# A two-layer trunk on one core: both token halves in one 512-column product, and a rebuilt start

## The chip, the cores and the metric

The kernel runs on one core of a Trainium2 chip. The metric is the device time of one execution in microseconds. Before the change it is 1028.43 us, the median of three runs (1027.76 to 1029.43). The engines are named as in the profile: PE multiplies matrices (PEld is its loading of the stationary operand), DVE and ACT work elementwise, POOL does a few small things, and SP issues most of the transfers.

## The reference, cut to what matters

There are 256 tokens of width 1024 and two layers. Each layer is a feed-forward block, a mixer with two kinds of attention, and a second feed-forward block. All of it is float32.

```
mod = silu(c) @ ada_w[l] + ada_b[l]            # nine rows of 1024 per layer: shift, scale, gate
h = rmsnorm(x, norm_pre[l, 0]) * (1 + sc1) + sh1
y = (silu(h @ w_gate) * (h @ w_up)) @ w_down    # 1024 -> 2816 -> 1024
x = x + 0.5 * g1 * rmsnorm(y, norm_post[l, 0])
# then the mixer with sh2, sc2, g2, then the second feed-forward block with sh3, sc3, g3
```

## The kernel before

**Products.** A float32 value is split into a high part `hi` and a rest `lo`, and a product of two such values is made of three products of the split parts (`mm3`, L476 to L478, and `mm3t`, L484 to L486). In `mm3` 128 tokens are stationary and 512 columns of a weight block move. In `mm3t` 128 columns of a weight block are stationary and the 256 tokens move: weight hi by tokens hi (L484), weight hi by tokens lo (L485), weight lo by tokens hi (L486). The transposed tokens lie in two tiles `hTh` and `hTl`. Every weight block comes by DMA into a `raw` tile and is split in pieces by ACT (`hi`, L437) and DVE (`lo`, L438).

**A feed-forward block** (`ffn`). Its first 512 hidden columns are made with `mm3` from `rows_of`, one token half at a time; in the very first block the loop at the program's start does it. The other 2304 come in nine steps `j` of 256 columns. A step takes a gate block and an up block of 1024 x 256 each, and for both makes 2 x 8 triples of 256-column products into one PSUM tile (`w_a` or `w_b`). Then ACT takes silu of the gate tile (L640), DVE multiplies it by the up tile (L641), and ACT and DVE split the result (L634, L635). The down products (`mm3`, 24 per 256 hidden columns) run between. PSUM has eight tiles: two of each of the tags `w0`, `w1`, `a` and `b`.

**Modulation in the background.** The rows of `ada_w` that are not needed at once are streamed behind the main work. DVE sums them by the values of silu(c) (L501), PE adds over the partitions (L519 and the line before it).

**The start.** Shift and scale of the first block are needed before any real product. They come in four quarters `q` of 256 columns: for each, a shift block and a scale block of 1024 x 256 are loaded (`eraw`). For each, PE makes 16 products that go to 32 partitions each (L959), DVE adds the bias row (L962), one product with `sel` adds up and spreads to all partitions (L963), DVE scales and shifts the tokens (L971, L972), PE transposes them (L591), ACT and DVE write `hTh` (L594) and `hTl` (L595), and 24 products of the first weight blocks follow. Until then PE runs products that nobody uses (`warm`, L937), in numbers given by `WARM`.

**Order.** Nothing of the order is left to the program text. `keep_order` builds the dependences, plays the program forward with a length for every instruction (`cost`), goes backward from the end for due times, repeats this a few times, and fixes the best order found on each engine, SP's queue of transfers included. Numbers in `shift` and `START_ORDER` move whole groups.

Of the kernel before, what the change touches and what calls it, by code (L numbers as in the profile page):

```python
# [11 lines left out]
F32R = mybir.dt.float32r  # L12
# [3 lines left out]
P = 128  # L16
D = 1024
# [13 lines left out]
START_ORDER = ['s0 x0 s1 c0 g0 x1 c1 f0 s2 f1', 'c2 g1 f2 s3 c3 f3', '', '', '']  # L31
WARM = [2, 5, 2]
# [18 lines left out]
def cost(ins, eng, slots):  # L51
# [3 lines left out]
    if kind == "InstDMACopy":  # L55
        return 4 * free * ins.outs[0].ap[0][1] / 360
# [17 lines left out]
    return 264 if kind == "InstTensorScalarPtr" else 464  # L74


def keep_order(tc, nc, slots, shifts):
# [20 lines left out]
    for k, ins in enumerate(L):  # L98
        touch = []
        for w, lst in ((False, ins.ins), (True, ins.outs)):  # L100
            for x in lst:
# [5 lines left out]
                lo = 0 if space == "PSUM" else b.offset if space == "DRAM" else b.offset % row  # L107
                hi = 1 << 30
                if space != "PSUM":
                    hi = lo + 1 + sum(abs(s) * (c - 1) for s, c in (ap if space == "DRAM" else ap[1:]))  # L110
                touch.append((w, name, lo, hi))
# [184 lines left out]
def trunk(ctx, tc, x, c, rel_bias, ada_w, ada_b, norm_pre, norm_post, w_gate, w_up,  # L296
# [125 lines left out]
    def load(shape, srcs):  # L422
        raw = praw.tile([P, 2048], F32, tag="raw", name=nm("raw"))
        rv = raw.rearrange("p (a b) -> p a b", a=shape[0])
# [4 lines left out]
    def unit(key, shape, src, uses=1):  # L429

        if key not in units:
# [3 lines left out]
            for z in range(sec["split"]):  # L435
                sl = slice(z * 2048 // sec["split"], (z + 1) * 2048 // sec["split"])
                nc.scalar.activation(hi[:, sl], raw[:, sl], AF.Copy)  # L437
                nc.vector.tensor_sub(lo[:, sl], raw[:, sl], hi[:, sl].bitcast(F32))  # L438
            units[key] = [uses, hi.rearrange("p (a b) -> p a b", a=shape[0]),
                          lo.rearrange("p (a b) -> p a b", a=shape[0])]  # L440
# [38 lines left out]

    def mm3t(ps_, kt, wt, sl, start, stop):  # L480

        wh, wl = wt[0][:, kt, sl], wt[1][:, kt, sl]
        hh, hl = hT[0][:, :, kt, :], hT[1][:, :, kt, :]
# [93 lines left out]
    hT = [ctile([P, 2, KT, P], f"hT{n}", F32R) for n in "hl"]  # L577
# [8 lines left out]
    def to_T(h, k0, nk, src, turned=False):  # L586
# [5 lines left out]
        hi, lo = (hT[n][:, h, k0:k0 + nk, :] for n in range(2))  # L592
# [51 lines left out]
    def rows_of(h, pair, get):  # L644

        for p_, g in zip(pair, get):
            for q in range(2):
                w = g(q)
                for k in range(4):
                    kt = q * 4 + k  # L650
                    mm3(p_, hT[0][:, h, kt, :], hT[1][:, h, kt, :], w, k, slice(0, 512), kt == 0, kt == 7)
# [8 lines left out]
    def ffn(l, i, first):  # L660
# [21 lines left out]
        for j in range(9):  # L682
# [365 lines left out]
```

## Time and profile before

| | |
|---|---|
| median of three runs | 1028.43 us |
| profiled execution | 1027.23 us |
| its span | 1025.5 us |
| PE, PEld busy | 1005.2, 893.9 us |
| DVE, ACT, POOL busy | 800.5, 553.5, 42.0 us |
| DMA read | 259.76 MB, 254 GB/s over the span |

The span reaches from the first to the last instruction; 1.7 us of the execution lie outside it. Busy times are the union of an engine's instructions; a product of PE is shown longer than its distance to the next, since products are pipelined.

### The profile page before, as it was taken

Reading aid. Unit: us, or ns where it says so; the run is one execution under the profiler, and the core shown is the slowest. Engines: PE = TensorE matmul, PEld = TensorE weight load, DVE = VectorE, ACT = ScalarE, POOL = GpSimd, SP = SyncE. Lnnn points to the kernel's source line nnn. Section 1 sums busy time; section 2 is a strip of 40 time slices with the busy share of each in tenths; the row PEclk is TensorE's granted clock in tenths of the full one; section 3 lists DMA queues with packets and bytes.
Section 4 is the critical chain, followed back from the end, with each engine's and each line's share of the span. In section 5 each row is a group of like instructions: output and inputs, shape, how many; then the busy total and the mean of one; then the engine's idle time right before and its main releaser. Section 6 shows DMA issues by size and latency. Waiting matters only on the chain. (4 is left out here: it accounts for less than half of the span.)

```text
span 1025.5 us, 17316 instructions
## 1 busy us (share of the span) xinstructions
PE 1005.2 (98%) x6514; PEld 893.9 (87%) x6514; DVE 800.5 (78%) x1493; ACT 553.5 (54%) x1250; POOL 42.0 (4%) x80
## 2 busy tenths in 40 slices
PE   7999999999999999999999999999999999999997
PEld 3699998978887899999979999998798779999996
DVE  4799888978887898798889888886879788555542
ACT  2456443665677665555465445444477766544431
POOL 1000000020002000000010000000100110000000
PEclk9999999999999999999999999999999999999999
DMA  9999998958994588898839887886589638555511
GB/s 328 365 361 325 313 284 295 343 175 279 311 306 168 207 291 295 285 316 311 290 122 308 298 290 284 303 288 226 168 301 323 209 127 272 193 181 189 184 64 41
DMA packets 171855, 261.95 MB, mean 255 GB/s; under 512 B 6396, under 2 KB 107484, under 8 KB 171772
## 3 DMA queue, kind: packets, MB, share of 16 engines
q1 hardware_dynamic: 171616, 260.78, 75.3%
q8 instruction: 51, 0.84, 0.3%
q14 instruction: 32, 0.26, 0.1%
q10 hardware_dynamic: 156, 0.07, 0.0%
HBM read 259.76 MB, written 1.07 MB: 254 GB/s over the span
## 5 line engine op out<-in xcount | busy, mean ns | idle before, releaser
L438 DVE TENSOR_TENSOR lo_a<-raw_a,hi_a 128x512 fp32r<-128x512 f32 (+1 forms) x540 | 294.1, 593 | 43.9 <-issue 23.4
L437 ACT ACTIVATE hi_a<-raw_a 128x512 fp32r<-128x512 f32 (+1 forms) x540 | 259.9, 547 | 123.3 <-PE w_a L485 25.7
L484 PE MATMUL w_a<-hTh,hi_a 128*128 128x256 f32 x768 | 218.9, 285 | 0.6 <-ACT kz_a L733 0.6
L485 PE MATMUL w_a<-hTl,hi_a 128*128 128x256 f32 x768 | 217.8, 284 | 0.0
L486 PE MATMUL w_a<-hTh,lo_a 128*128 128x256 f32 x768 | 217.3, 283 | 0.0
L484 PEld LDWEIGHTS w_a<-hTh,hi_a 128*128 128x128 f32 x768 | 147.1, 192 | 2.2 <-ACT kz_a L733 0.8
L485 PEld LDWEIGHTS w_a<-hTl,hi_a 128*128 128x128 f32 x768 | 147.1, 192 | 1.2 <-issue 0.3
L486 PEld LDWEIGHTS w_a<-hTh,lo_a 128*128 128x128 f32 x768 | 147.0, 191 | 0.4
L485 PE MATMUL w_b<-hTl,hi_b 128*128 128x256 f32 x512 | 144.8, 283 | 0.0
L484 PE MATMUL w_b<-hTh,hi_b 128*128 128x256 f32 x512 | 144.8, 283 | 0.0
L486 PE MATMUL w_b<-hTh,lo_b 128*128 128x256 f32 x512 | 144.7, 283 | 0.0
L437 ACT ACTIVATE hi_b<-raw_b 128x512 fp32r<-128x512 f32 (+1 forms) x224 | 105.1, 544 | 71.3 <-DMA raw_b<-in_ffn_w_up_dram 16.5
L438 DVE TENSOR_TENSOR lo_b<-raw_b,hi_b 128x512 fp32r<-128x512 f32 (+1 forms) x224 | 119.9, 588 | 22.9 <-issue 17.1
L484 PEld LDWEIGHTS w_b<-hTh,hi_b 128*128 128x128 f32 x512 | 98.1, 192 | 1.0
L485 PEld LDWEIGHTS w_b<-hTl,hi_b 128*128 128x128 f32 x512 | 98.1, 192 | 0.9
L486 PEld LDWEIGHTS w_b<-hTh,lo_b 128*128 128x128 f32 x512 | 98.1, 192 | 0.2
L501 DVE SCALAR_TENSOR_TENSOR acc_a<-araw_a,ccol,acc_a 128x512 f32<-128x512 f32 x110 | 82.2, 747 | 12.5 <-DMA araw_a<-in_ada_w_dram 11.0
L477 PE MATMUL a_b<-lo_a,str_a 128*128 128x512 f32 x156 | 60.8, 392 | 0.0
L476 PE MATMUL a_b<-hi_a,str_a 128*128 128x512 f32 x156 | 60.3, 392 | 0.0
L478 PE MATMUL a_b<-hi_a,str_a 128*128 128x512 f32 x156 | 60.2, 390 | 0.0
L501 DVE SCALAR_TENSOR_TENSOR acc_b<-araw_b,ccol,acc_b 128x512 f32<-128x512 f32 x46 | 34.5, 749 | 6.4 <-DMA araw_b<-in_ada_w_dram 5.5
L478 PE MATMUL w_b<-hi_a,hTl 128*128 128x512 f32 (+1 forms) x96 | 36.5, 380 | 0.0
(245 smaller groups left out, 1723.8 us busy)
## 6 DMA issues: line engine op xcount, KB each, us to landing
araw_a<-in_ada_w_dram SPq DMA_DIRECT2D x84, 512.0 KB
raw_a<-in_ffn_w_down_dram SPq DMA_DIRECT2D x30, 1024.0 KB
raw_a<-in_ffn_w_gate_dram SPq DMA_DIRECT2D x26, 1024.0 KB
raw_a<-in_ffn_w_up_dram SPq DMA_DIRECT2D x26, 1024.0 KB
araw_b<-in_ada_w_dram SPq DMA_DIRECT2D x44, 512.0 KB
raw_a<-in_mix_w_in_dram SPq DMA_DIRECT2D x18, 1024.0 KB
raw_b<-in_ffn_w_gate_dram SPq DMA_DIRECT2D x16, 1024.0 KB
raw_b<-in_ffn_w_up_dram SPq DMA_DIRECT2D x16, 1024.0 KB
```

Source lines behind the costliest of these rows:

```text
L437: nc.scalar.activation(hi[:, sl], raw[:, sl], AF.Copy)
L438: nc.vector.tensor_sub(lo[:, sl], raw[:, sl], hi[:, sl].bitcast(F32))
L476: nc.tensor.matmul(ps_, hh, wh, start=start, stop=False)
L477: nc.tensor.matmul(ps_, hh, wl, start=False, stop=False)
L478: nc.tensor.matmul(ps_, hl, wh, start=False, stop=stop)
L484: nc.tensor.matmul(ps_, wh, hh, start=start, stop=False)
L485: nc.tensor.matmul(ps_, wh, hl, start=False, stop=False)
L486: nc.tensor.matmul(ps_, wl, hh, start=False, stop=stop)
L501: nc.vector.scalar_tensor_tensor(acc[:, :n], raw[:, t, :], ccol[:, k:k + 1], b if t == 0 else acc[:, :n], op0=ALU.mult, op1=ALU.add)
```

## The change

Four things are edited.

1. `hTh` and `hTl` become one tile `hT`, in which the high and the low part of a 128-row slice lie side by side. The new `mm2t` multiplies weight hi by both at once (512 columns), and weight lo by the high part (256 columns). The two sums lie in two halves of a PSUM tile of their own for each 128 hidden columns; ACT copies the one half out, DVE adds the other. It is used in all steps `j` of the four feed-forward blocks but the very first one.
2. At the start the first quarter of modulation is summed with 16 products that write all 128 partitions, with no `sel` product and no DVE addition; its four half blocks are loaded by themselves.
3. The gate and up block of step `j` = 0 of the first block are loaded in quarters at the start (`b0` to `b3`), and multiplied with each quarter of the tokens as it comes. Their two PSUM tiles (`ahead`) are held from the start on. `WARM` falls from 2, 5, 2 to 2, 3, 0.
4. `cost` gets other lengths for products, transfers and POOL's instructions, and `keep_order` sees strided accesses more finely, so that the order changes everywhere. The memsets of the mixer's key tile are cut in four.

```diff
-START_ORDER = ['s0 x0 s1 c0 g0 x1 c1 f0 s2 f1', 'c2 g1 f2 s3 c3 f3', '', '', '']
-WARM = [2, 5, 2]
+START_ORDER = ['s0 x0 s1 c0 g0 x1 c1 f0 b0 s2 f1', 'b1 c2 g1 f2 s3 c3', 'b2 f3', 'b3', '']
+WARM = [2, 3, 0]
...
-            return max(free, 256) / 2.4 + 2.5
-        whole = max(4 * free / 2.4 + 4, 160)
+            return free / 2.4 + 13.5
+        whole = max(4 * free / 2.4 + 8, 222)
...
+    def mm2t(ps_, k, wt, sl):
+        for kt in range(k):
+            wh, wl = wt[0][:, kt, sl], wt[1][:, kt, sl]
+            both = lambda **f: nc.tensor.matmul(ps_, wh, hTa[:, kt], **f)
+            if kt < k - 1:
+                both(start=kt == 0, stop=False)
+            nc.tensor.matmul(ps_[:, :256], wl, hT[0][:, kt], start=False, stop=False)
+            if kt == k - 1:
+                both(start=kt == 0, stop=True)
...
-            pair = (wps(), wps())
-            for p_, (tag, ws) in zip(pair, (("g", w_gate), ("u", w_up))):
-                w = u_both(l, f, ws, tag, j)
-                for t in range(2):
-                    for k in range(KT):
-                        mm3t(p_[:, t * 256:(t + 1) * 256], k, w, slice(t * P, (t + 1) * P), k == 0, k == KT - 1)
-            act = split(swiglu(*pair), 512)
+            if first and j == 0:
+                hm = swiglu(*ahead)
+            else:
+                gu = []
+                for b, (tag, ws) in enumerate((("g", w_gate), ("u", w_up))):
+                    w = u_both(l, f, ws, tag, j)
+                    gu.append(st())
+                    for t in range(2):
+                        p_ = wps(b)
+                        mm2t(p_, KT, w, slice(t * P, (t + 1) * P))
+                        dst = gu[b][:, t * 256:(t + 1) * 256]
+                        nc.scalar.activation(dst, p_[:, 256:], AF.Copy)
+                        nc.vector.tensor_add(dst, p_[:, :256], dst)
+                nc.scalar.activation(gu[0], gu[0], AF.Silu)
+                nc.vector.tensor_mul(gu[0], gu[0], gu[1])
+                hm = gu[0]
+            act = split(hm, 512)
...
+            if q == 0:
+                nc.tensor.matmul(both, sel[0:1, :], fl(brow0[0:1, 0]), start=True, stop=False)
             for z in range(2):
                 for k in range(KT):
+                    if q == 0:
+                        nc.tensor.matmul(both[:, z * 256:(z + 1) * 256], ccol[:, k:k + 1].to_broadcast([P, P]),
+                                         pre[q][z][:, k, :], start=False, stop=z == 1 and k == KT - 1)
+                        continue
...
+        with shift(START_NEXT):
+            for n in range(2):
+                for t in range(2):
+                    for k in range(2):
+                        kt = q * 2 + k
+                        wh, wl = (w[i][:, n * 2 + k, t * P:(t + 1) * P] for i in range(2))
+                        p_ = ahead[n][:, t * 256:(t + 1) * 256]
+                        nc.tensor.matmul(p_, wh, hT[0][:, kt], start=kt == t == 0, stop=False)
+                        nc.tensor.matmul(p_, wh, hT[1][:, kt], start=False, stop=False)
+                        nc.tensor.matmul(p_, wl, hT[0][:, kt], start=False, stop=kt == 7 and t == 1)
```

The start on PE, before: `a_b` from `gb` and `x` are the unused products, `eraw` are modulation blocks, `hi` and `lo` the first weight block.

```order
L937 MATMUL a_b_138<-gb,ident 128x512 x2
L364 MATMUL w_a_110<-ident,c_105 128x8
L937 MATMUL a_b_138<-x_119,ident 128x512 x5
L959 MATMUL w_a_203<-eraw_a_148,ccol 32x256 x8
L959 MATMUL w_a_203<-eraw_a_153,ccol 32x256 x8
L963 MATMUL w_a_204<-st_a_221,str_a_139 128x512
L937 MATMUL a_b_138<-x_120,ident 128x512
L591 MATMUL w_a_227<-ident,st_a_224 128x128
L959 MATMUL w_a_290<-eraw_a_151,ccol 32x256 x8
L591 MATMUL w_a_227<-ident,st_a_224 128x128
L937 MATMUL a_b_138<-x_120,ident 128x512
L476 MATMUL a_a_135<-hi_a_232,hTh 128x512
```

The same place after the change.

```order
L981 MATMUL a_b_137<-gb,ident 128x512
L376 MATMUL w_a_110<-ident,c_105 128x8
L981 MATMUL a_b_137<-gb,ident 128x512
L981 MATMUL a_b_137<-x_119,ident 128x512 x3
L1005 MATMUL w_a_205<-erow_a_144,str_a_138 128x512
L1009 MATMUL w_a_205<-eraw_a_147,ccol 128x256 x8
L1009 MATMUL w_a_205<-eraw_a_153,ccol 128x256 x8
L618 MATMUL w_a_226<-ident,st_a_223 128x128 x2
L618 MATMUL w_b_258<-ident,st_b_255 128x128 x2
L489 MATMUL a_a_134<-hi_a_231,hT 128x512
L490 MATMUL a_a_134<-lo_a_232,hT 128x512
L491 MATMUL a_a_134<-hi_a_231,hT 128x512
```

The first quarter's products write 128 partitions and are followed by the transposes of both token halves; the second quarter's first block (`eraw_a_151`) no longer stands ahead of the first real product.

ACT at the start after the change: `raw_a_161` is the first weight block, `raw_a_164` the first quarter `b0`, `hT` the transposed tokens.

```order
L627 ACTIVATE junk,ss_a_186<-x_119 128x512 x2
L627 ACTIVATE junk,ss_a_196<-x_120 128x512 x2
L450 ACTIVATE hi_a_231<-raw_a_161 128x512 x4
L450 ACTIVATE hi_a_275<-raw_a_164 128x256 x2
L621 ACTIVATE hT<-w_a_226 128x2x128
L621 ACTIVATE hT<-w_b_258 128x2x128
```

The tokens' `hT` now stands behind all four pieces of the first weight block and the gate half of `b0`; before, two pieces of the first block stood ahead of it.

PE in a step `j` of the first feed-forward block, before: one hidden tile `w_a_902`, three products a slice.

```order
L484 MATMUL w_a_902<-hTh,hi_a_906 128x256
L485 MATMUL w_a_902<-hTl,hi_a_906 128x256
L486 MATMUL w_a_902<-hTh,lo_a_907 128x256
L484 MATMUL w_a_902<-hTh,hi_a_906 128x256
L485 MATMUL w_a_902<-hTl,hi_a_906 128x256
```

PE in such a step after the change.

```order
L498 MATMUL w_b_1140<-hT,hi_b_1111 128x512
L501 MATMUL w_b_1140<-hT,lo_b_1112 128x256
L498 MATMUL w_b_1140<-hT,hi_b_1111 128x512
L501 MATMUL w_b_1140<-hT,lo_b_1112 128x256
L498 MATMUL w_b_1140<-hT,hi_b_1111 128x512
```

Two products a slice take the place of three, with as many columns in all.

DVE beside that, after the change: L726 is the new addition, L451 the splitting of weight blocks, L526 the background sums.

```order
L726 TENSOR_TENSOR st_b_1139<-w_b_1140,st_b_1139 128x256
L451 TENSOR_TENSOR lo_a_1231<-raw_a_1228,hi_a_1230 128x512 x3
L726 TENSOR_TENSOR st_b_1070<-w_b_1090,st_b_1070 128x256
L526 SCALAR_TENSOR_TENSOR acc_a_1387<-araw_b_1437,ccol,acc_a_1387 128x512
L726 TENSOR_TENSOR st_b_1139<-w_b_1159,st_b_1139 128x256
```

The additions are strewn between the splits and the sums; each stands for one PSUM tile.

## Rows read from the trace of the kernel before

**Rows 1.** The page: engine, busy us, share of the span, instructions.

```profile
PE 1005.2 (98%) x6514; PEld 893.9 (87%) x6514; DVE 800.5 (78%) x1493; ACT 553.5 (54%) x1250; POOL 42.0 (4%) x80
```

**Rows 2.** Windows: length, busy us (instructions) by engine, clock, DMA share, GB/s.

```profile
0.00:19.00 19.00, 14.41 (x72) 5.77 (x72) 5.38 (x11) 5.88 (x13) 3.50 (x15) 1.00 0.96 314
19.00:22.00 3.00, 2.25 (x21) 1.08 (x21) 2.92 (x7) 0.67 (x2) 0.00 (x0) 1.00 1.06 379
22.00:64.00 42.00, 42.00 (x271) 32.60 (x271) 34.11 (x62) 21.20 (x41) 0.29 (x1) 1.00 1.06 359
64.00:221.00 157.00, 156.06 (x1055) 144.13 (x1054) 136.16 (x213) 80.21 (x152) 2.01 (x4) 1.00 0.92 314
...
341.00:520.00 179.00, 178.54 (x1202) 165.31 (x1201) 156.53 (x354) 100.30 (x282) 1.77 (x4) 1.00 0.84 285
...
534.00:716.00 182.00, 181.91 (x1216) 168.38 (x1217) 149.09 (x235) 90.03 (x170) 2.19 (x4) 1.00 0.83 287
...
835.00:1004.00 169.00, 168.60 (x1156) 156.79 (x1155) 97.80 (x156) 77.71 (x142) 0.71 (x2) 1.00 0.52 175
```

**Rows 3.** PE's waits in 64:221: who for whom, us, times, longest.

```profile
PE w_a L519 <- DVE ast_a L517: 0.9, 1, 0.9
```

**Rows 4.** The same in 341:520.

```profile
PE w_b L591 <- DVE st_b L613: 0.5, 1, 0.5
```

**Rows 5.** The page's groups: busy us, mean ns.

```profile
L484 PE MATMUL w_a<-hTh,hi_a 128*128 128x256 f32 x768 | 218.9, 285 | 0.6 <-ACT kz_a L733 0.6
...
L484 PE MATMUL w_b<-hTh,hi_b 128*128 128x256 f32 x512 | 144.8, 283 | 0.0
```

**Rows 6.** Timeline of PE in 100:112: start us, us.

```profile
99.70 0.40 PE L476 MATMUL a_b<-hi_a,str_a 128*128 128x512 f32 x1
...
105.15 0.28 PE L484 MATMUL w_b<-hTh,hi_b 128*128 128x256 f32 x1
...
108.98 0.28 PE L486 MATMUL w_b<-hTh,lo_b 128*128 128x256 f32 x1
```

**Rows 7.** Timeline of DVE in 350:372.

```profile
349.64 4.44 DVE L438 TENSOR_TENSOR lo_a<-raw_a,hi_a 128x256 fp32r<-128x256 f32 x13
```

**Rows 8.** Lines of DVE, 256 columns from PSUM: busy us, mean ns, idle before.

```profile
L972 DVE TENSOR_TENSOR st_a<-st_a,w_a 128x256 f32<-128x256 f32 x4 | 1.7, 421 | 0.1
```

**Rows 9.** The same of ACT.

```profile
L817 ACT ACTIVATE st_a<-w_a 128x256 f32<-128x256 f32 x16 | 6.1, 380 | 4.6 <-PE w_a L815 4.6
```

**Rows 10.** DVE's waits in 64:221.

```profile
DVE acc_a L501 <- DMA araw_a<-in_ada_w_dram: 4.9, 4, 3.1
DVE acc_b L501 <- DMA araw_a<-in_ada_w_dram: 3.8, 3, 2.4
DVE lo_a L438 <- ACT hi_a L437: 3.5, 2, 2.0
```

**Rows 11.** DVE's waits in 341:520.

```profile
DVE st_a L641 <- PE w_a L486: 5.3, 4, 3.0
```

**Rows 12.** Timeline of all engines in 0:22.

```profile
6.56 4.56 PE L937 MATMUL a_b<-x,ident 128*128 128x512 f32 x10
...
11.14 1.93 PE L959 MATMUL w_a<-eraw_a,ccol 128*32 128x256 f32 x32
...
13.97 1.10 PE L963 MATMUL w_a<-st_a,str_a 128*128 128x512 f32 x2 [0.90 <-DVE st_a L962]
...
17.18 1.07 PE L959 MATMUL w_a<-eraw_a,ccol 128*32 128x256 f32 x16
...
18.54 0.39 ACT L594 ACTIVATE hTh<-w_a 128x256 fp32r<-128x256 f32 x1
...
18.98 0.61 PE L476 MATMUL a_a<-hi_a,hTh 128*128 128x512 f32 x1
...
20.71 1.07 PE L959 MATMUL w_a<-eraw_a,ccol 128*32 128x256 f32 x16
...
21.71 0.63 ACT L437 ACTIVATE hi_a<-raw_a 128x512 fp32r<-128x512 f32 x1 [0.51 <-DMA raw_a<-in_ffn_w_up_dram]
...
21.71 0.50 PE L476 MATMUL a_b<-hi_a,hTh 128*128 128x512 f32 x1
```

More of the change, by code (lines that the diff above doesn't have):

```diff
@@ L55, in cost @@
     if kind == "InstDMACopy":
-        return 4 * free * ins.outs[0].ap[0][1] / 360
+        run = 1
+        for step, n in reversed(list(ins.ins[0].ap)):
+            if step != run and n > 1:
+                break
+            run *= n
+        return 4 * free * ins.outs[0].ap[0][1] / (348 if run <= 256 else 388 if run <= 512 else 415)
     if kind == "InstMatmult":
@@ L106, in keep_order @@
                 ap, space = list(x.ap), slots[name][2]
[L107 to L111, printed above, removed]
+                if space == "PSUM":
+                    touch.append((w, name, 0, 1 << 30))
+                    continue
+                lo = b.offset if space == "DRAM" else b.offset % row
+                dims = [(s, c) for s, c in (ap if space == "DRAM" else ap[1:]) if c > 1]
+                starts = [lo]
+                while len(dims) > 1 and dims[0][0] > 0 and len(starts) * dims[0][1] <= 16:
+                    s, c = dims.pop(0)
+                    starts = [v + s * n for v in starts for n in range(c)]
+                low, size = sum(min(0, s * (c - 1)) for s, c in dims), sum(abs(s) * (c - 1) for s, c in dims)
+                touch += [(w, name, v + low, v + low + size + 1) for v in starts]
         for w, name, lo, hi in touch:
@@ L429, in unit @@
     def unit(key, shape, src, uses=1):
+        size = shape[0] * shape[1]
         if key not in units:
@@ L575, in rstd_of @@
         return r2
-    hT = [ctile([P, 2, KT, P], f"hT{n}", F32R) for n in "hl"]
+    hTa = ctile([P, KT, 2, 2, P], "hT", F32R)
+    hT = [hTa[:, :, n] for n in range(2)]
     def back(t):
@@ L896, in ada_load @@
         raw = (plo if m else phi).tile([P, KT, 256], F32, tag="lo" if m else "hi", name=nm("eraw"))
-        nc.sync.dma_start(raw, rows(ada_w[0], 0, KT)[:, :, m * D + q * 256:m * D + (q + 1) * 256])
+        n = KT // 2 if q == 0 else KT
+        for k in range(0, KT, n):
+            nc.sync.dma_start(raw[:, k:k + n], rows(ada_w[0], k * P, n)[:, :, m * D + q * 256:m * D + (q + 1) * 256])
         return raw
@@ L908, in load_first, with load_next @@
         loaded["first", q] = load((4, 512), first_srcs(q))
+    def load_next(q):
+        loaded["next", q] = load((4, 256), [(slice(n * 2, n * 2 + 2), rows(w[0, 0], q * 256, 2)[:, :, 512:768])
+                                            for n, w in ((0, w_gate), (1, w_up))])
     def load_mod(q, m):
@@ L939, in trunk @@
     warm(WARM[0], gb)
+    ahead = (wps(0), wps(1))
     rx, xg = [None, None], [[None, None], [None, None]]
@@ L960, in trunk @@
                                      pre[q][z][:, k, :], start=k < 4, stop=k >= 4)
-            t = st()
-            nc.vector.tensor_add(t, parts, fl(brow0[:, q]))
-            nc.tensor.matmul(both, sel, t, start=True, stop=True)
+            if q:
+                t = st()
+                nc.vector.tensor_add(t, parts, fl(brow0[:, q]))
+                nc.tensor.matmul(both, sel, t, start=True, stop=True)
         cq = slice(q % 2 * 256, q % 2 * 256 + 256)
```

37 lines of the change are left out of this document (22 added, 15 removed).

## The prediction

> **What bounds the kernel now.** I read the page's busy times first, then windows by stage, then PE's waits, then timelines. PE is busy 98% of the span and DVE 78% [rows 1]. The windows show what the share hides: in the four feed-forward stages (64 to 221, 341 to 520, 534 to 716, 835 to 1004) PE is busy for all but 0.1 to 0.9 us, while DVE is busy 136.16 of 157, 156.53 of 179, 149.09 of 182 and 97.80 of 169 us [rows 2]. PE's waits there are one of 0.9 us in the first stage and one of 0.5 in the second [rows 3, 4]. So in these stages time is what PE's products take, one after another; DVE is next, with 21, 22, 33 and 71 us of room. From 22 to 64 PE is busy too, 42.00 of 42 us, with DMA at a share of 1.06; only before 22 does PE wait for data [rows 2].
>
> **The new product.** A product's cost is its distance to the next, not its shown duration. From 99.70 to 105.15 there are 24 products of 512 columns, 227.1 ns each; from 105.15 to 108.98 32 distances of 256-column products, 119.7 ns each [rows 6]. A line through the two gives 0.4195 ns a column and 12.3 ns that every product pays. A triple of three products costs 359.1 ns now and 227.1 + 119.7 = 346.8 after: 12.3 ns less. There are 768 + 512 = 1280 triples [rows 5]; 128 of the mixers and the 32 of the first step `j` = 0 keep the old form, which leaves 1120. 1120 x 12.3 ns = 13.8 us off PE (3.1 in the first stage, 3.5 in each of the other three). Since PE has no other time to lose there, this is also on the path. The columns stay the same; that a 512-column product takes 227 ns with the tokens moving and the weights stationary no row shows. Bounds: if it costs as much as 512 columns do in two pieces, 239.4 ns, nothing is gained; if it costs what the line gives without the fixed part, 214.8 ns, 27.6 us are. I take 227.1, a row of the same engine, type and size.
>
> The row puts the fixed part of a product at 12.3 ns. The Trainium skill, page "TensorE: Matmul & The Clock Gate", section "Back-to-back issue gap", gives columns divided by 2.4 plus about 2.5 ns for a product at full clock. This trace does not agree: it would be 109 ns where the rows have 119.7. By the page the term would be 1120 x 2.5 ns = 2.8 us.
>
> **What the new form adds.** For each of the 2 x 2 tiles of a step ACT copies 256 columns out of PSUM and DVE adds 256: 32 tiles in the first stage, 36 in each of the others, 140 in all. DVE's 13 pieces of 256 columns took 4.44 us, 0.335 apart and 0.42 the last [rows 7]; from PSUM the duration is the same, 0.421 [rows 8]. So 10.7 us more on DVE in the first stage and 12.1 in the others, 47 in all. ACT's copy of this size takes 0.380 [rows 9], 12 to 14 us a stage; ACT is busy about half of every stage [rows 2], so it costs nothing by occupancy. The silu and the multiplication stay one each.
>
> Does DVE hold it? Room after the addition and PE's shorter stage: 20.8 - 10.7 - 3.1 = 7.0 us, 22.5 - 12.1 - 3.5 = 6.9, 32.9 - 15.6 = 17, 71.2 - 15.6 = 56. In the last two it is covered. In the first two DVE is then busy 96% of the time, and some of its room is not free: in the first stage it waits 4.9 and 3.8 us for modulation rows and 3.5 for ACT [rows 10], in the second 5.3 for PE's tile [rows 11]. The waits for modulation shrink when DVE is later, and those sums are due only at a stage's end; those for PE's tile are now spread over four tiles a step. The additions stand between splits of weight blocks, and PE has blocks ahead, so that a late addition first eats that lead. Bounds: nothing lost, or all of 10.7 + 12.1 + 12.1 in three stages. I take 1.5 us, near the low end, since PE waited 1.4 us in two stages in which DVE was busy 87%.
>
> The addition's other wait is PE's: the next product into a PSUM tile waits for the copy and the addition of that tile. With two tiles a tag and 24 down products or another pair of tiles between, that is 2.6 us or more of cover against 0.4 + 0.4. In the first steps one tile of each tag is still held by `ahead`; there the two halves of a block follow each other through one tile, twice or three times, at up to 0.8 us. It is in the 1.5.
>
> **The start.** Before, the first quarter's 16 products begin at 11.14, the `sel` product at 13.97, `hT` is written at 18.54, and the first real product starts at 18.98, alone; the stream runs from 21.71, when the up half of the first block has landed and ACT splits it [rows 12]. By then both halves of the second quarter's modulation (17.18 and 20.71, 1.07 us each) are done too.
>
> After: an unused 512-column float32 product takes 4.56 / 5 = 0.91 us [rows 12], so a 256-column one 0.46. Three from 6.56, the bias row, and 16 of 0.46 end at 6.56 + 4 x 0.91 + 7.3 = 17.5. DVE's two passes at 0.42 and the transposes bring `hT` to 19.1 at best. But on ACT it stands behind the gate half of `b0`. In SP's queue the bytes to that half are: tokens 1.05 MB, modulation 2.10 + 1.05, gain 0.26, first block 1.05, `b0` 0.26, small ones 0.07, together 5.84 MB; at 314 GB/s that is 18.6 us [rows 2]. The same count for the kernel before (6.62 MB, 20.7 us) lies 1.0 before the split at 21.71, so 19.6 here, and two pieces at 0.38 and `hT` at 0.39 let the first real product start at 20.8. Behind it are two modulation groups (2.14) and one product (0.23) that the kernel before had done at 21.71: 20.8 + 2.4 = 23.2, or 1.5 us later. The quarters `b0` to `b3` only move 96 products forward, since PE had no gap from 22 on to fill [rows 2]; they cover the chain of the next quarter. Bounds: -0.5 if `b0` lands early enough that `hT` goes at 19.1, and +4.4 if a megabyte more stands ahead (1.05 MB at 359 GB/s is 2.9).
>
> The fewer unused products, the memsets in four and POOL's lengths cost nothing: POOL is busy 4% [rows 1], and the unused ones run while data are on the way. The new lengths in the planner move the mixers' order; nothing in a row prices that, and I put it at 0, within 3 either way.
>
> **Sum.** The profiled execution took 1027.2 us, span 1025.5 and 1.7 around it. 1027.2 - 13.8 + 1.5 + 1.5 = 1016.4. The median of the runs is 1.2 above that execution, so the forecast is 1017.6.
>
> **The rivals.**
> 1. *DVE's queue becomes the clock* (slower). Where an addition stands in front of a split that PE needs, PE waits for both. For: 96% in two stages. Against: 21 and 22 us of room that PE did not feel. If half of the 35 us in the first three stages shows, 1027.2 - 13.8 + 1.5 + 17.5 = 1032.4, with 1.2 1033.6; if all does, 1051. It decides from the point where over 12.3 us show (a third). Taken at a half to all of it: 1037. Chance 0.08.
> 2. *The fixed part goes with the columns or the weight's columns, not with the product.* Then a 512-column product with the tokens moving takes up to 239.4 ns and the triple saves nothing or a fifth: 1027.2 - 0 + 3.0 + 1.2 = 1031.4, or 1028.6 at a fifth (2.8 us). For: no row has this form. Against: the two sizes of [rows 6], each with its own weight load. The rule of the Trainium skill's page "TensorE: Matmul & The Clock Gate" named above leads to the same 2.8 us. Chance 0.06, half of it within 0.2%.
> 3. *All covers hold.* The start loses nothing, DVE loses nothing, and the mixers' new order gives 3: 1027.2 - 13.8 - 0.5 - 3 + 1.2 = 1011.1. For: PE never waited at DVE's 87%. Against: the order of ACT at the start. Chance 0.14.
>
> That the products are not paired is excluded: 1120 of either kind stand in PE's order.
>
> **How the numbers follow.** Forecast 0.72, rivals 0.08, 0.06 and 0.14. The forecast's own range is 1012 to 1024 (start -0.5 to +4.4, DVE 0 to 6, mixers 3 either way, not all at once). The range is 1009 to 1026: it takes in rival 3 and what of the forecast has a larger DVE term. This kernel's measurement tells 0.2%, 2.1 us, from no change. Faster by more: 0.72 + 0.14, less 0.02 for the forecast's far end, 0.84; within: 0.02 + 0.03 = 0.05; slower: 0.08 + 0.03 = 0.11.
>
> **What would show it.** Right: distances of 227 and 120 ns in the pairs; feed-forward stages shorter by 3 to 4 us each with PE's waits under 2; DVE over 93% in the first two; the first real product near 20.8 and the stream after. Wrong: pairs at 350 ns or more; PE waiting for splits behind L726; the last feed-forward stage, where DVE has room, not shorter by 3.5.

## The result, and the profile after

The changed kernel takes 1040.22 us (median of four runs, 1038.96 to 1041.38) beside 1028.1 us of the kernel before on the same chip. The ratio is 1.0127, 95% interval [1.0105, 1.0148]: it is slower by 1.3%. The profiled execution took 1039.74 us with a span of 1038.0.

The page's line of busy times, to be read beside [rows 1]:

```profile
PE 1004.7 (97%) x5386; PEld 840.7 (81%) x5386; DVE 846.6 (82%) x1640; ACT 597.9 (58%) x1398; POOL 44.7 (4%) x92
```

PE has 1128 products fewer and is busy 0.5 us less in a span that is 12.5 us longer. DVE has 46 us more, as forecast. PE's idle time, the span less its busy time, grows from 20.3 to 33.3 us: the loss is time in which PE waits. What the products save does not show in its busy time either; the run `e8` below, with the same products in another order, has 999.1 us.

The windows of the kernel after, with the columns of [rows 2]. The first stage now reaches to 235:

```profile
19.00:22.00 3.00, 1.13 (x5) 0.66 (x6) 1.36 (x4) 2.30 (x6) 0.00 (x0) 0.82 1.10 348
22.00:28.00 6.00, 6.00 (x15) 4.70 (x16) 3.11 (x8) 0.72 (x2) 0.00 (x0) 0.52 1.08 362
28.00:64.00 36.00, 35.66 (x259) 27.32 (x259) 26.89 (x55) 15.34 (x35) 2.33 (x1) 1.00 1.02 334
64.00:235.00 171.00, 163.12 (x840) 136.23 (x839) 152.99 (x257) 96.50 (x198) 2.32 (x4) 1.00 0.87 294
...
845.00:1014.00 169.00, 168.47 (x879) 143.31 (x878) 116.88 (x200) 92.73 (x184) 2.49 (x4) 1.00 0.54 181
```

In the first stage PE is idle 7.9 of 171 us, where it was idle 0.9 of 157. DVE is busy 89% there, not 96%. Where the stages end is seen from ACT's first squares of the second token half behind each of the six blocks (two layers of feed-forward, mixer, feed-forward). They start at 221.9, 334.0, 526.2, 719.0, 828.6 and 1017.9 us in the kernel before and at 233.8, 350.0, 541.0, 732.6, 843.7 and 1030.4 after. So the six parts, the first with the start in it, differ by +11.9, +4.1, -1.2, -1.2, +1.5 and -2.6 us: 16.0 us are lost up to the end of the first mixer, and 3.5 come back later.

PE's waits in 64:235 after, who for whom, us, times, longest (before: [rows 3]):

```profile
PE w_b L543 <- DVE st_b L726: 2.4, 1, 2.4
PE w_b L498 <- DVE st_a L726: 1.6, 2, 1.0
PE w_a L498 <- DVE row_b L557: 1.3, 1, 1.3
PE w_a L498 <- ACT row_a L554: 1.3, 1, 1.3
PE w_a L543 <- DVE st_a L726: 0.8, 1, 0.8
```

Of the 7.9 us, 5.1 stand behind an addition (L726). One wait of 1.05 us followed back, in the timeline of all engines from 175 to 178 us (start, length, engine, what, idle before and its releaser):

```profile
175.74 0.63 ACT L450 ACTIVATE hi_b<-raw_b 128x512 fp32r<-128x512 f32 x1 [7.22 <-DMA raw_b<-in_ffn_w_up_dram]
176.27 0.37 ACT L725 ACTIVATE st_a<-w_a 128x256 f32<-128x256 f32 x1
...
176.67 0.42 DVE L726 TENSOR_TENSOR st_a<-w_a,st_a 128x256 f32<-128x256 f32 x1 [2.15 <-ACT st_a L725]
...
177.15 0.50 PE L498 MATMUL w_b<-hT,hi_b 128*128 128x512 f32 x1 [1.05 <-DVE st_a L726]
```

ACT stands 7.22 us at a weight piece that has not landed. The copy out of PSUM is behind it in ACT's fixed order, DVE's addition behind the copy, and PE's next product behind the addition. PE's wait names DVE, but the late thing is a transfer and the order in which ACT was told to take it. One link further back is SP, which issued that transfer (timeline of SP):

```profile
168.20 0.37 SPq L438 DMA_DIRECT2D raw_b<-in_ffn_w_up_dram  x1
```

What SP's queue waited for from 166 to 169 us:

```profile
SPq L438 <- DVE lo_a L451: 2.0, 1, 2.0
```

The transfer could start only when DVE's split of an older weight block (L451) had freed its buffer. So the chain comes back to DVE, and the trace alone doesn't say which of the three engines is late first.

The products themselves. Timeline of PE, three tiles of eight pairs in a row:

```profile
900.24 0.63 PE L498 MATMUL w_a<-hT,hi_a 128*128 128x512 f32 x2
...
904.35 0.40 PE L498 MATMUL w_a<-hT,hi_a 128*128 128x512 f32 x1
904.59 0.28 PE L501 MATMUL w_a<-hT,lo_a 128*128 128x256 f32 x1
904.70 0.40 PE L498 MATMUL w_a<-hT,hi_a 128*128 128x512 f32 x1
...
908.70 0.40 PE L498 MATMUL w_a<-hT,hi_a 128*128 128x512 f32 x1
```

From 900.24 to 908.70 are 24 pairs: 352.5 ns each. Over the whole trace the median from a 512-column product to the next is 235 ns and from a 256-column one 117 to 118, while the 512-column products of `mm3` still take 227. A pair saves 6.6 ns on the triple's 359.1 by these timelines, 7.5 by the medians (3 x 120 less 352.5), and not 12.3.

The start, timeline of all engines:

```profile
19.66 1.76 ACT L450 ACTIVATE hi_a<-raw_a 128x512 fp32r<-128x512 f32 x4 [3.13 <-DMA raw_a<-in_ffn_w_up_dram]
...
21.33 0.36 ACT L621 ACTIVATE hT<-w_a 128x256 fp32r<-128x256 f32 x1
...
21.74 0.80 PE L489 MATMUL a_a<-hi_a,hT 128*128 128x512 f32 x1 [1.13 <-ACT hT L621]
...
23.19 0.63 PE L489 MATMUL a_a<-hi_a,hT 128*128 128x512 f32 x1
...
27.83 0.39 PE L491 MATMUL a_b<-hi_a,hT 128*128 128x512 f32 x1
28.06 0.39 PE L489 MATMUL a_b<-hi_a,hT 128*128 128x512 f32 x1
```

ACT's split starts at 19.66. The forecast had 19.6 for the gate half of `b0`; what starts here is the up half of the first weight block, and `b0` follows. So four pieces stand ahead of `hT` and not two, and the first real product starts at 21.74 and not 20.8. PE had done only four transposes in the 3 us before, and its granted clock is 0.82 in 19:22 and 0.52 in 22:28. The products lie 0.43 us apart until 27.46, and 0.23 from 27.83 on.

### The profile page after: what moved, and what is told of

The parts are those of the page before. It is cut to its first block, busy times and chain, and to the rows that moved or that the text cites. A ratio compares the mean times of both kernels' runs of the same rounds, so it can differ in the third digit from the quotient of the medians.

```text
span 1038.0 us, 15309 instructions
## 1 busy us (share of the span) xinstructions
PE 1004.7 (97%) x5386; PEld 840.7 (81%) x5386; DVE 846.6 (82%) x1640; ACT 597.9 (58%) x1398; POOL 44.7 (4%) x92
## 5 line engine op out<-in xcount | busy, mean ns | idle before, releaser
L451 DVE TENSOR_TENSOR lo_a<-raw_a,hi_a 128x512 fp32r<-128x512 f32 (+1 forms) x548 | 296.3, 586 | 25.9 <-PE w_b L501 8.0
L498 PE MATMUL w_a<-hT,hi_a 128*128 128x512 f32 x608 | 213.2, 398 | 2.7 <-DVE row_b L557 1.3
L498 PE MATMUL w_b<-hT,hi_b 128*128 128x512 f32 x512 | 180.4, 398 | 2.6 <-DVE st_a L726 1.6
L501 PE MATMUL w_a<-hT,lo_a 128*128 128x256 f32 x608 | 158.5, 281 | 0.0
L450 ACT ACTIVATE hi_b<-raw_b 128x512 fp32r<-128x512 f32 (+1 forms) x224 | 106.5, 544 | 47.7 <-DMA raw_b<-in_ffn_w_up_dram 19.6
L501 PE MATMUL w_b<-hT,lo_b 128*128 128x256 f32 x512 | 133.4, 281 | 0.0
L451 DVE TENSOR_TENSOR lo_b<-raw_b,hi_b 128x512 fp32r<-128x512 f32 (+1 forms) x224 | 122.3, 588 | 12.9 <-PE w_a L501 5.5
L498 PEld LDWEIGHTS w_a<-hT,hi_a 128*128 128x128 f32 x608 | 110.8, 188 | 24.8 <-DVE row_b L557 1.6
L501 PEld LDWEIGHTS w_a<-hT,lo_a 128*128 128x128 f32 x608 | 114.8, 189 | 6.7
L498 PEld LDWEIGHTS w_b<-hT,hi_b 128*128 128x128 f32 x512 | 93.7, 188 | 22.2 <-DVE st_a L726 2.2
L501 PEld LDWEIGHTS w_b<-hT,lo_b 128*128 128x128 f32 x512 | 96.6, 189 | 6.4 <-issue 0.6
L526 DVE SCALAR_TENSOR_TENSOR acc_a<-araw_a,ccol,acc_a 128x512 f32<-128x512 f32 x115 | 85.8, 746 | 9.2 <-DMA araw_a<-in_ada_w_dram 8.1
L726 DVE TENSOR_TENSOR st_a<-w_a,st_a 128x256 f32<-128x256 f32 x76 | 31.7, 419 | 18.2 <-ACT st_a L725 18.0
L509 PE MATMUL w_a<-hT,hi_a 128*128 128x256 f32 x128 | 37.1, 292 | 0.0
L489 PE MATMUL w_a<-hi_a,hT 128*128 128x512 f32 (+1 forms) x96 | 36.4, 379 | 0.5 <-DVE hT L622 0.5
```

What stands on the lines that cost most here:

```text
L489: nc.tensor.matmul(ps_, hh, wh, start=start, stop=False)
L498: both = lambda **f: nc.tensor.matmul(ps_, wh, hTa[:, kt], **f)
L501: nc.tensor.matmul(ps_[:, :256], wl, hT[0][:, kt], start=False, stop=False)
L509: nc.tensor.matmul(ps_, wh, hh, start=start, stop=False)
L526: nc.vector.scalar_tensor_tensor(acc[:, :n], raw[:, t, :], ccol[:, k:k + 1], b if t == 0 else acc[:, :n], op0=ALU.mult, op1=ALU.add)
L726: nc.vector.tensor_add(dst, p_[:, :256], dst)
```

## The experiments

All were timed against the kernel before on the same chip; the ratio and its 95% interval are to that kernel. "To the first mixer's end" is the second of the six marks above: the start, the first feed-forward block and the first mixer. "Pieces" are DVE's modulation sums (`scalar_tensor_tensor` of 128 x 512) in 150 to 235 us of the span. These two columns are of one profiled execution each, which in e21 is 7.5 us above the median and in e17 3.3 below.

| kernel | median us | ratio, interval | to the first mixer's end | pieces |
|---|---|---|---|---|
| before | 1026.8 to 1028.2 | 1 | 334.0 | 18 |
| e27 before, a transpose 1 ns longer | 1026.3 | 0.9986 [0.9975, 0.9997] | 335.3 | 21 |
| e25 before, matmul lengths new | 1047.3 | 1.0194 [1.0179, 1.0209] | 347.9 | 32 |
| e1 before, all lengths new | 1050.9 | 1.0221 [1.0194, 1.0248] | 352.3 | 37 |
| e3 after, with triples | 1055.6 | 1.0263 [1.0238, 1.0288] | 353.8 | 35 |
| after | 1040.2 | 1.0127 [1.0105, 1.0148] | 350.0 | 24 |
| e2 after, old start | 1043.0 | 1.0141 [1.0110, 1.0171] | 350.6 | 22 |
| e6 after, one run of 512 | 1041.7 | 1.0138 [1.0109, 1.0166] | 346.5 | 24 |
| e13 after, old DMA lengths | 1040.4 | 1.0135 [1.0117, 1.0154] | 349.7 | 24 |
| e15 after, old POOL lengths | 1048.6 | 1.0206 [1.0177, 1.0235] | 355.8 | 24 |
| e23 after, more lead | 1048.0 | 1.0208 [1.0174, 1.0241] | 350.3 | 24 |
| e14 after, old matmul lengths | 1032.2 | 1.0058 [1.0037, 1.0079] | 340.5 | 17 |
| e8 after, all lengths old | 1025.3 | 0.9983 [0.9968, 0.9997] | 337.4 | 18 |
| e17 e8, both matmul lengths new | 1045.7 | 1.0185 [1.0162, 1.0208] | 348.8 | 24 |
| e30 e8, float32r length new | 1036.2 | 1.0101 [1.0067, 1.0135] | 349.3 | 24 |
| e31 e8, fp32 length new | 1030.9 | 1.0045 [1.0028, 1.0063] | 339.1 | 18 |
| e18 e8, products 8 ns shorter | 1030.4 | 1.0022 [1.0006, 1.0039] | 340.4 | 18 |
| e20 e8, old start | 1029.6 | 1.0020 [1.0007, 1.0033] | 338.3 | 15 |
| e21 e8, other half | 1026.8 | 1.0004 [0.9983, 1.0025] | 341.0 | 19 |
| e16 pairs, all else before | 1078.5 | 1.0497 [1.0477, 1.0517] | 356.3 | 16 |

**Which part of the change.** `e1_planner_only` puts part 4 of the change alone into the kernel before, the finer record and the memsets included (these lines show the lengths):

```diff
-        return 4 * free * ins.outs[0].ap[0][1] / 360
+        return 4 * free * ins.outs[0].ap[0][1] / (348 if run <= 256 else 388 if run <= 512 else 415)
-            return max(free, 256) / 2.4 + 2.5
-        whole = max(4 * free / 2.4 + 4, 160)
+            return free / 2.4 + 13.5
+        whole = max(4 * free / 2.4 + 8, 222)
-    return 264 if kind == "InstTensorScalarPtr" else 464
+    return 300 if kind == "InstTensorScalarPtr" else 570 if free == 1 else 170 + 0.76 * free
```

> The kernel before with part 4 of the change alone: the new lengths and the finer view of accesses in the planner, and the key tile's memsets in four. Same products, same start. Theory ORDER (the new lengths make a worse order everywhere, of the 12 us a good part): 1033 to 1040 us. Theories ACT (the new PSUM copies stand on ACT behind weight pieces whose transfer is late) and DVE (the additions fill DVE, so buffers and transfers come late) both expect 1026 to 1031, with the first feed-forward stage as long as before (post-norm of the second half at about 222 us).

It is 22.7 us slower than before. PE's waits in its 64:235:

```profile
PE w_b L495 <- ACT bq L415: 8.2, 1, 8.2
PE a_b L487 <- ACT str_a L645: 6.4, 1, 6.4
```

The products there are the old ones; the order alone costs more than the whole change, and more than any of the theories had. `e2_old_start` takes parts 2 and 3 out of the kernel after, `e3_triples` part 1:

```diff
-START_ORDER = ['s0 x0 s1 c0 g0 x1 c1 f0 b0 s2 f1', 'b1 c2 g1 f2 s3 c3', 'b2 f3', 'b3', '']
+START_ORDER = ['s0 x0 s1 c0 g0 x1 c1 f0 s2 f1', 'c2 g1 f2 s3 c3 f3', '', '', '']
```

> The changed kernel with the start of before (parts 2 and 3 undone: first quarter through the sel product, block j = 0 in the loop, the old list of loads and unused products). Theory START (PE idles from 18.4 to 21.7, its granted clock falls to 0.50 until 28, and hT stands behind b0 on ACT: 5 to 6 us) expects 1034 to 1035, with the feed-forward stage's waits of PE still there. If the PSUM tiles that are held from the start also cause those waits, 1028 to 1030. If the start costs nothing, 1040.

The intervals of e2 and after overlap: the start decides nothing here. In e2 the clock was full through it, but fell to 0.50 at three later places.

```diff
-                        p_ = wps(b)
-                        mm2t(p_, KT, w, slice(t * P, (t + 1) * P))
+                        mm3t(p_[:, t * 256:(t + 1) * 256], k, w, slice(t * P, (t + 1) * P), k == 0, k == KT - 1)
```

> The changed kernel with part 1 undone in the loop: three 256-column products a slice into one PSUM tile, silu and multiplication straight from PSUM, no copy and no addition; one tile for the tokens, the new start and the planner stay. Theories ACT and DVE: PE's waits in the feed-forward stages go (first stage 8 us) and 8 us of product time come back in all; with the start's loss of 5 to 6 left, 1032 to 1036. Theory ORDER: PE's waits stay and the triples add 8, 1045 or more.

Without the pairs the kernel after takes 15.4 us more. The pairs are a gain under these lengths, more than their products save; under the old lengths they are none (e20, below).

**Which lengths.** `e8_old_lengths` is the kernel after with the three old lines of `cost` (the diff above backward); `e13_old_dma`, `e14_old_pe` and `e15_old_pool` put back one kind each.

> The kernel after with every length in the planner's table of costs as before (DMA, matmul, fp32 matmul and GpSimd), the finer record of tiles, the pairs and the new start kept. Theory LENGTHS (the lengths alone make the order bad, 22 us in the kernel before): 1040 less about 22, 1013 to 1022 us, and the waits of the products for the gate and up additions and splits in 64:235 go back to about 3 us. Rival PAIR ORDER (with pairs the planner puts the copies and additions badly under any lengths): 1034 to 1042 us, the waits stay near 8 us. Rival TOUCH (the finer record of tiles did it): unchanged, 1040 us.

> The kernel after with the transfers' length alone as before (bytes by one rate of 360 for every run length). Theory RATES (348, 388 and 415 promise pieces too early, so ScalarE's queue holds the first half of a weight piece ahead of copies and splits that are due; longest wait of ScalarE for a raw piece 7.2 us): 1015 to 1025 us, and that longest wait falls under 4 us. Rival MATMUL LENGTHS (the products planned longer, 119.9 and 226.8 instead of 109.2 and 215.8, leave no reserve): unchanged, 1036 to 1044 us.

> The kernel after with the matmuls' lengths alone as before (109.2 ns for 256 columns, 215.8 for 512, fp32 at least 160). Theory MATMUL LENGTHS (a shorter planned product keeps the splits and weight pieces further ahead of TensorE): 1015 to 1025 us, waits of TensorE for additions, splits and lo pieces in 64:235 near 3 us instead of 8. Theory RATES: unchanged, 1036 to 1044 us.

> The kernel after with GpSimd's lengths alone as before (264 and 464 ns). Both theories on lengths: no part of the loss, 1037 to 1043 us. Rival SCATTER (any change in the table gives another order, and times fall some us to either side by chance): somewhere between 1030 and 1050, away from 1040 by more than 3 us.

The lengths together are 14.9 us (1040.2 to 1025.3), less than the theory of e8 had. The transfers' length does nothing, the matmuls' gives 8 us, less than forecast, and POOL's alone, put back, costs 8.3: in this order a few microseconds either way belong to no length. Much of it shows in PE's clock. Windows of e15 (columns of [rows 2]):

```profile
176.00:184.00 8.00, 6.02 (x18) 4.52 (x19) 6.71 (x13) 5.02 (x11) 0.00 (x0) 0.57 0.75 270
323.00:331.00 8.00, 7.46 (x26) 5.59 (x27) 4.99 (x12) 3.79 (x13) 1.80 (x4) 0.57 0.40 118
```

The granted clock of e15 falls to 0.50 in five places (0.57 is the mean of each window shown), during about 22 us of PE's busy time. An estimate of the loss is half of that, 11 us, since a 512-column product takes 0.43 us at that clock and 0.23 at the full one. By the same count it is 3 us in after, 10 in e23, and nothing in before, e8 and e20 (the last microseconds, where PE is done, left out). Of the 10.0 us by which e15's span is longer than that of after, only 1.2 are idle time of PE. PE's waits in 64:235 of e8, to be set beside those of after:

```profile
PE w_b L493 <- ACT hi_b L445: 2.0, 1, 2.0
PE w_a L496 <- DVE lo_a L446: 1.4, 2, 1.1
PE w_a L484 <- DVE hT L617: 1.0, 1, 1.0
PE w_a L493 <- DVE row_b L552: 0.4, 1, 0.4
```

No addition (L721 there) is among them, with the same 140 additions on DVE; 1.4 us are waits for DVE's splits. The page's line of e8:

```profile
PE 999.1 (98%) x5386; PEld 838.3 (82%) x5386; DVE 846.7 (83%) x1640; ACT 600.8 (59%) x1398; POOL 41.3 (4%) x92
```

**Length or chance.** `e17_new_pe` sets the two matmul lines new in e8, `e25_before_pe` in the kernel before. `e18_short_pe` goes the other way (`free / 2.4 - 5.5`). `e27_before_110` plans a transpose at 110 ns for 109 in the kernel before, which changes no instruction, only their order.

> The kernel with pairs and old lengths (1025.3 us) with the matmuls' new lengths alone (free / 2.4 + 13.5, fp32 at least 222). Theory MATMUL LENGTHS (longer planned products leave the split and evacuation work without lead): 1033 to 1042 us, the step of 8 us that taking them out of the kernel after gave, or more. Rival SCATTER (any new order falls within some 8 us by chance, as GpSimd's lengths alone moved it): 1018 to 1033, either side of 1025.

> The kernel with pairs and old lengths (1025.3 us) with the matmuls planned 8 ns shorter still (free / 2.4 - 5.5: 101.2 ns for 256 columns, 207.8 for 512). Theory MATMUL LENGTHS: at least as good, 1016 to 1026 us, since the other engines are planned further ahead. Rival SCATTER: anywhere in 1018 to 1035, with no relation to the length.

> The kernel before with the matmuls' lengths alone as in the kernel after (119.9 ns for 256 columns, 226.8 for 512, fp32 at least 222). Theory MATMUL LENGTHS: most of the 22.7 us that the whole new table cost there, 1042 to 1052 us. Rival SCATTER: slower than before, since before's order is a picked one, but by any amount, 1030 to 1050. Rival OTHER LENGTHS (DMA and GpSimd did it): 1025 to 1031.

> The kernel before with one length in the planner changed by 1 ns (a transpose by TensorE 110 instead of 109), which means nothing for what the chip does; the order differs in some 300 of 6075 rows of TensorE. Theory SCATTER AROUND A PICKED ORDER: 1033 to 1050 us, as with the other changes of the table. Theory MATMUL LENGTHS (a systematic effect): 1025 to 1031 us, no change to be measured.

In e27 a changed order is no slower, against theory SCATTER AROUND A PICKED ORDER; but it is one small change, and e15 moved by 8.3 us. The new matmul lengths cost 20 us in either kernel (1047.3 - 1027.5 and 1045.7 - 1025.3), more than any other change of a length, so they are a cause. That shorter is better still falls with e18: it is 4 to 5 us slower than e8. Whether a longer product costs as such, or any length other than the one beside which the other numbers of the planner were chosen, these runs don't part. `e30_f32r_only` and `e31_fp32_only` part them:

```diff
-            return max(free, 256) / 2.4 + 2.5
+            return free / 2.4 + 13.5
```
```diff
-        whole = max(4 * free / 2.4 + 4, 160)
+        whole = max(4 * free / 2.4 + 8, 222)
```

> The kernel with pairs and old lengths (1025.3 us) with the float32r products alone planned as in the kernel after (119.9 and 226.8 ns, which is what the trace shows for them). Theory FLOAT32R (a plan in which TensorE is slower lets the others come later): 1038 to 1048 us, with the loss in the feed-forward stages too. Rival FP32 (it is the attention's products, planned twice as long as they are): 1023 to 1030 us.

> The kernel with pairs and old lengths with the fp32 products alone planned as in the kernel after (4 free / 2.4 + 8, at least 222 ns instead of at least 160; the trace shows 112 ns from one 128x64 product to the next). Theory FLOAT32R: 1023 to 1030 us. Rival FP32: 1033 to 1046 us, with the loss in the two mixers (3 to 7 us each) and little in the feed-forward stages.

The float32r length costs 10.9 us and fp32's 5.6; together they cost 20.4. Both fall short of what their theories had (1038 and 1033 at the least). That the fp32 loss lies in the mixers holds: its two mixers take 10.1 us more than e8's and its first feed-forward block 2.9 less. That the float32r loss lies in the feed-forward blocks doesn't: 9.2 of the 13.5 us by which e30's span is longer than e8's lie in the first mixer, where PE is idle 9.1 us (e8: 2.0), 2.7 in the start and the first feed-forward block.

**What the longer products do to the order.** The column of pieces parts the kernels without exception: 15 to 21 wherever float32r has its old length or a shorter one, 22 to 24 with pairs and 32 to 37 with triples where it has the new. But 235 us is another place of the program in each kernel. Windows of DVE's modulation lines alone up to the mark that ends the first feed-forward block (length, DVE busy us and pieces, clock, DMA share, GB/s of the core), before, e25, e8 and after:

```profile
0.00:221.90 221.90, 50.78 (x68) 1.00 0.95 322
```
```profile
0.00:230.90 230.90, 59.81 (x80) 0.99 0.96 323
```
```profile
0.00:227.20 227.20, 47.59 (x64) 1.00 0.91 305
```
```profile
0.00:233.80 233.80, 50.67 (x68) 0.99 0.91 306
```

Up to the same place the new lengths bring 12 pieces more into the kernel before (e25) and 4 more into the kernel with pairs (after against e8); after has as many as before. Each piece needs 0.262 MB of `ada_w` (128 x 512 x 4 bytes). Twelve are 3.1 MB, or 10 us of transfers at 323 GB/s, where e25's block ends 9.0 us later; four are 1.0 MB, or 3.4 us at 306 GB/s, where that of after ends 6.6 us later than e8's. The rate of the transfers is the same within each two. The whole program has 256 pieces in every kernel. What waits is the weights, and behind them ACT, as in the timeline at 175.74. In e25 it is one wait of 6.8 us for ACT's writing of the mixer's bias (`bq`, L404), behind a weight piece for which ACT waited 5.0. PE's clock falls with it, too (windows with the columns of [rows 2]):

```profile
140.00:150.00 10.00, 3.23 (x13) 1.62 (x12) 8.19 (x13) 4.82 (x12) 0.00 (x0) 0.84 0.96 329
150.00:160.00 10.00, 10.00 (x70) 10.00 (x71) 9.96 (x17) 3.53 (x7) 0.00 (x0) 0.81 0.82 287
```

That the float32r length moves the pieces is shown. That they make the loss is argued from their bytes, and only for the first feed-forward block: no kernel holds them back with the new lengths, e31, e15 and e23 lose time without more of them, and what the new lengths cost in the mixers is not followed here.

**More lead instead.** `e23_lead` keeps the new lengths and raises two of the planner's waiting times:

```diff
-("DVE", "PE"): 235, ... ("Activation", "PE"): 275,
+("DVE", "PE"): 435, ... ("Activation", "PE"): 475,
```

> The kernel after with its new lengths, and two of the planner's waiting times raised by 200 ns: from VectorE to TensorE 235 to 435 and from ScalarE to TensorE 275 to 475, so that what feeds TensorE is planned earlier. Theory LEAD (the longer matmuls in the plan took lead from additions and splits): 1022 to 1032 us, and the waits of TensorE for additions and splits in 64:235 fall from 8 us to under 4. Rival SCATTER: 1032 to 1050, with waits in other places.

It is slower than after, by 7.8 us: theory LEAD falls. The pieces stay at 24.

**What the pairs are worth.** `e20_old_start_old_lengths` is e8 with the start of before; `e16_pairs_alone` has also the old record of tiles and memsets.

> The kernel with pairs, finer tile record and old lengths (1025.3 us) with the start as before too: what the pairs are worth with no other part of the change. If the start is worth its 3 us that the fetch and the evacuations promised: 1027 to 1030 us. If it costs, as the first product for the gate being later says: 1020 to 1024 us. Theory SCATTER: outside both by more than 3 us.

> The kernel before with the pairs alone (one product of 512 columns and one of 256 in place of three of 256, copy and addition from PSUM); lengths, tile record, memsets and start as before. Theory LENGTHS (the loss of the change sits in the planner's new lengths, 1050.9 against 1028.2 in the kernel before): the pairs by themselves are a gain, 7.4 ns x 1120 = 8.3 us less than before, 1017 to 1022 us. Rival PAIRS COST (the 47 us of additions on VectorE make waits that eat the products' saving under any lengths): 1026 to 1034 us. With the new start and the old lengths 1025.3 was measured, so a result near 1019 would also price that start at 6 us.

e20 has the pairs and the finer record with the start and the lengths of before, and it is 0.2% slower than before: by themselves the pairs with that record bring nothing. PE is busy 6.1 us less in it (999.1 for 1005.2), but idle 5.7 more. e8 is 0.2% faster than before: with the old lengths the new start is worth 3.8 us (0.0037 of 1027), with intervals that don't meet. Yet its own block ends 2.5 us later (227.2 in e8, 224.7 in e20), so the gain lies in the order of later stages. e16 missed both theories. PE's longest waits in its whole span:

```profile
PE w_b L607 <- DVE st_b L629: 18.7, 5, 6.0
PE w_a L607 <- DVE st_a L629: 16.1, 4, 6.5
PE w_a L478 <- DVE hT L611: 5.6, 2, 3.7
```

L607 is the transpose into the next `hT`, L629 and L611 are on the way to it. The old record takes a strided access for everything from its first to its last address, so that the high and the low part, interleaved in one tile, look like one. e16 and e20 differ in the record and the memsets alone, and 49 us lie between them: the finer record belongs to the pairs.

**Why a pair takes 352 ns.** `e6_flat` gives the moving tokens as one run of 512 in the kernel after, `e21_other_half` lets the low product add into the half that the high product wrote first last:

```diff
-            both = lambda **f: nc.tensor.matmul(ps_, wh, hTa[:, kt], **f)
+            both = lambda **f: nc.tensor.matmul(ps_, wh, hTa[:, kt].rearrange("p a b c -> p (a b c)"), **f)
```
```diff
-            nc.tensor.matmul(ps_[:, :256], wl, hT[0][:, kt], start=False, stop=False)
+            nc.tensor.matmul(ps_[:, 256:], wl, hT[0][:, kt], start=False, stop=False)
```

> The changed kernel with the moving operand of the 512-column product written as one run of 512 in place of 2 x 2 x 128 (same memory, same order of instructions). In the changed kernel that product takes 234.7 ns to the next and the 256-column one 117.4, where 227.1 and 119.7 were forecast. If the form of the access costs the 7 ns, 227 and 1120 x 7 = 8 us less: 1032. If the 7 ns come from the change of length between neighbours or of weights, nothing moves: 1040 and 234.7.

> The kernel with pairs and old lengths, with the product of the low weights accumulated into columns 256 to 511 of the same tile instead of 0 to 255; same sum, same order on every engine. Theory SAME COLUMNS (the 512-column product waits some 7 ns where it begins in the columns that the product just before wrote): its time to the next product goes from 234.7 to about 227 ns and the kernel gains 1120 x 7 ns = 8 us, 1017 us. Rival WEIGHT LOAD (the 512 is followed by a new set of weights behind a short product, whatever the columns): 234.7 and 117.3 ns stay, 1025 us.

Neither moves a product: 234 and 117 ns in both, here eight pairs of e21 in 2.82 us:

```profile
900.48 0.63 PE L493 MATMUL w_a<-hT,hi_a 128*128 128x512 f32 x2
...
903.30 0.40 PE L493 MATMUL w_a<-hT,hi_a 128*128 128x512 f32 x1
```

The form of the operand and the columns written are not the reason. What is stays open.

## Why the prediction was wrong

The step that failed is "The new lengths in the planner move the mixers' order; nothing in a row prices that, and I put it at 0, within 3 either way." They cost 14.9 us in the kernel after; in the kernel before all of part 4 costs 22.7, and e17, e25, e30 and e31 show that the lengths of PE's products are what costs. Nor are the mixers the only place: of e1's 24.8 us of span 18.6 lie in the start and the first feed-forward block, and of the 16.0 between e8 and after 6.6 lie there, 8.8 in the two mixers.

That is not all. With the old lengths the same change takes 1025.3 us, just inside the stated range of 1009 to 1026 and 7.7 over the forecast: 1.8 us faster than before by the ratio, where 10.8 were forecast. A second step failed with it, "Since PE has no other time to lose there, this is also on the path": in e20 PE is busy 6.1 us less and idle 5.7 more.

The other terms, by the prediction's steps:

- *Products, -13.8.* The mechanism was right, the size was off: 227.1 was taken for the 512-column product and 235 came, so a pair saves 6.6 to 7.5 ns, and 1120 pairs 7.4 to 8.4 us. The last stage, where nothing else waits, is 2.6 us shorter after and 1.7 to 3.1 in the other kernels with pairs and the finer record, which is less than the 3.5 named as the mark of failure.
- *Start, +1.5.* In its own block +1.0 (233.8 after, 232.8 in e2) and +2.5 (e8 against e20): about right there, though over the whole run e8 is 3.8 us under e20. The first real product came 0.9 us later than forecast, since ACT's order has all four pieces before `hT`, and the fallen clock took some 3 us from the 14 products up to 27.83, which I had not foreseen. That the block of after shows little of these beside e2 is chance: e2 loses as much to two falls of the clock later in the block, and in e8, with the new start, the clock stays at 1.00.
- *DVE's additions, +1.5.* DVE's addition took 0.419 us (0.421 forecast), ACT's copy 0.377 (0.380). The 1.5 for what PE loses by them was too small: without the new start and the new lengths (e20) the pairs and their additions leave PE idle 5.7 us more, and against the 7.4 to 8.4 us that the products save stand 7 to 8 us by its span (0.4 under that of before) and some 10 by its ratio of 1.0020. How much of it is the additions, and how much the order, no run parts.
- *Rival 1* named 1037 and waits of PE behind additions at L726; 1040 and 5.1 us of such waits came. Its mechanism is not borne out as stated: DVE is busy 89% of the first stage and not 96, and with the same additions e8 shows no wait for one. In the wait followed back DVE was late because ACT was, and ACT because of a transfer. A share of DVE's is not excluded, since that transfer had itself waited 2.0 us for a split.
- *Rival 2* is true in part. By the trace 7.4 to 8.4 of 13.8 us came. The Trainium skill, page "TensorE: Matmul & The Clock Gate", section "Back-to-back issue gap", would have given 2.8 us as an estimate, with the figure that it states for a product by itself and not for a stream with a weight load each; the trace lies between the two.

What misled me was the bound. The new float32r lengths are close to the rows (119.9 and 226.8 planned, 119.7 and 227.1 measured), and I took a truer plan for a harmless one. The new fp32 minimum is not even truer: it plans 222 ns for 160, where the mixers' 128x64 products lie 111 ns apart. My reading, which no run tests, is that the numbers in `shift` that place the modulation had been set beside products planned 11 ns too short, and no longer fit when those were put right.

## What to carry to other kernels

A planner's table is part of the tuning: a length that is nearer to the measured one can give a worse order. Price a change of the table as an unknown of its own, by 15 to 23 us here, and run it alone first. When you count background work in two orders, count up to the same place of the program and not to the same time. Look at the granted clock beside the waits, since a wait can be followed by products at half speed that count as busy. And when a wait names an engine that has time to spare, follow the chain until something has really not arrived, and then to what held back its issue.

## What the runs showed of the hardware

- A 512-column product with the tokens moving, alternating with a 256-column one, takes 235 ns to the next and the other 117, where each size among its own kind takes 227 and 120. The line through the latter two has 0.4195 ns a column, near the 0.4167 of one cycle at the granted clock of 1.00 (2.4 GHz). By one cycle a column they would be 213.3 and 106.7 ns, so 32 ns a pair are on top, 21 on the long and 11 on the short, against 40 on a triple. Why the long one pays more stays open (e6, e21).
- After PE had done only four transposes from 18.4 to 21.7 us its granted clock was 0.52 in 22:28 (the level of 1.2 GHz for nearly all of it), with PE busy all the while, and 1.00 after 28; 512-column products lay 0.43 us apart in the one and 0.23 in the other. In e25 it fell after 140 in a wait as well, and the window of 150:160 has 0.81. In e15 five such falls took about 11 us, by the estimate above.
- An order alone moves this kernel by more than its measurement tells: POOL's planned lengths by 8.3 us (e15) and two planned waiting times by 7.8 (e23), with the same work on every engine; most of either goes with the fallen clock. 1 ns on the transposes moved it by less than 2 (e27).
